# Feed-forwards: inverse deviations of the tokens applied to the up-projection's outputs instead of to the rows before the transposes

## The chip, the core and the metric

One core of one Trainium2 chip runs the whole program in one launch. The metric is the device time of an execution in microseconds (us), the median of several runs. The engines are named as the profile names them: PE (TensorE's matmuls), PEld (its weight loads), DVE (VectorE), ACT (ScalarE), POOL (GpSimd), SP (SyncE, which issues most transfers).

## What is computed

The reference runs 256 tokens of width 1024 through two models of two layers each, one after the other. Each layer is an attention and a feed-forward. The first two feed-forwards (`run_mlp`) are squared-ReLU MLPs. The last two (`run_ffn`) are what the change touches:

```
def conv_ffn(x, w_up, conv_w, conv_b, w_down):
    hdn = x @ w_up                       # 1024 -> 2 * 2816
    hdn = causal depthwise convolution of width 3 along the tokens(hdn) + conv_b
    gate, up = jnp.split(hdn, 2, axis=-1)
    return (jax.nn.gelu(gate, approximate=True) * up) @ w_down

h = h + rmsnorm(merge_heads(o) @ w_o, post_g)
f = conv_ffn(rmsnorm(h, ffn_pre_g[layer]), ...)
h = h + rmsnorm(f, ffn_post_g[layer])
```

`rmsnorm(h, g)` multiplies each token's row by its inverse deviation, 1 / sqrt(mean(h * h) + eps), and by the gain g. The inverse deviation is one number per token, so it can be applied before or after the matrix product; the convolution adds neighbouring tokens, so it must be applied before that.

## The kernel before

The tokens lie in two tiles of 128 (`t` = 0, 1). All weights are float32. A product is made of three matmuls in which each operand is split in a high and a low part: `split` (lines 162 to 190) writes the high part of a weight with ACT (`whi`, line 174) and the low part with DVE (`wlo`, line 175), a tile of 128x1024 at a time, in 8 buffers each.

`run_ffn` (lines 998 to 1023) does for each token tile: `op.run(t)`, the attention's output projection on PE; `add_post` (lines 492 to 503), which takes the inverse deviation of the projection's output and adds the normed rows to x (line 501); and `row_T` (lines 271 to 283), which multiplies x by the inverse deviation `x_rstd(t)` and by the gain's row (line 280, tile `y`), in two halves of 512 columns, and has PE transpose each half (`to_T`, line 257; evacuated by ACT at line 261, high part, and DVE at line 262, low part, tile `yT`). `x_rstd` (lines 232 to 245) is a chain: two squares with sums on ACT (line 236), two small DVE instructions (lines 238 and 240) and a power on POOL (line 222, tile `rstd`).

`conv_ffn` (lines 594 to 619) then goes through 11 groups `g` of 512 columns of the up-projection, two pairs (gate and up, `j` = 0, 1) of two chunks of 128 channels each. Group 0 goes through `up_tokens` (lines 533 to 549): the product with tokens on the partitions, an ACT copy out of PSUM (line 540, tile `ut`), PE transposes (line 543) and ACT copies (line 548). Groups 1 to 10 go through `up_pair` (lines 516 to 531): channels on the partitions, tokens along the row, evacuated by ACT (line 529) and DVE (line 530) into the tile `s`. The convolution follows: ACT scales and adds the bias (line 610, tile `cv`), DVE adds the two other taps (line 612, twice a chunk). Then come gelu (ACT, line 616), the product of gate and up (DVE, line 617) and the split of the result `u` (ACT line 512, DVE line 513). `Down` multiplies each `u` with the down-projection (lines 213 to 215) one group late, and takes the last three groups together at the end, tile t = 0 first, in the order 8, 9, 10.

The order of the instructions of each engine is laid out ahead of time by a scheduler that goes by the program's order and by when it reckons operands to be ready; each engine then runs its list strictly in order. Every 128x512 tile of the feed-forward's elementwise work comes from one pool of 5 buffers (tag `ev`).

`before_mlp` (lines 965 to 976), of the first two feed-forwards, already transposes rows that are multiplied by the gain alone (line 278) and takes the inverse deviation later. `along_rows` (lines 315 to 322) turns the two columns of inverse deviations into a row `R` of 256 on all partitions: two PE transposes (line 319) and a DVE copy (line 321); the attentions `layer_sb` and `layer_fox` use it.

Of the kernel before, what the change touches and what calls it, by code (L numbers as in the profile page):

```python
# [10 lines left out]
AF = mybir.ActivationFunctionType  # L11
ALU = mybir.AluOpType
PSUM = bass.MemoryType.PSUM

S, D, P = 256, 1024, 128
# [4 lines left out]
F2 = ((8 * D // 3 + 127) // 128) * 128  # L20
# [37 lines left out]
def body(ctx, tc, d, out):  # L58
    nc = tc.nc
    mm = nc.tensor.matmul  # L60
    act = nc.scalar.activation
    V = nc.vector
# [11 lines left out]
    def t512(name):  # L74
        return ap_.tile([P, 512], F32, name=name, tag="ev", bufs=E_BUFS)
# [7 lines left out]
    def acc_tile(i=0):  # L83

        tag = ("acc", "pt", "po")[i]
        return pp.tile([P, 512], F32, name="acc", tag=tag, bufs=1 if i else 2)

    def tp_tile(tag="ht"):
        return pp.tile([P, 4, P], F32, name="tp", tag=tag, bufs=2 if tag == "ht" else 1)

    def sc_tile():
        return pp.tile([P, 512], F32, name="sc", tag="sc", bufs=2)
# [20 lines left out]
    x = cst.tile([P, NT, D], F32, name="x")  # L113
# [118 lines left out]
    def row_rstd(lo, hi):  # L232

        ss = sm.tile([P, 2], F32, name="ss")
        for c, src in enumerate((lo, hi)):
            act(junk, src, AF.Square, accum_out=ss[:, c:c + 1])
        m0 = sm.tile([P, 1], F32, name="m0")
        V.tensor_scalar(m0, ss[:, 0:1], 1.0 / D, EPS, op0=ALU.mult, op1=ALU.add)
        ms = sm.tile([P, 1], F32, name="ms1")
        V.scalar_tensor_tensor(ms, ss[:, 1:2], 1.0 / D, m0, op0=ALU.mult, op1=ALU.add)  # L240
        return power(ms, 1)

    def x_rstd(t, src=None):
        src = x if src is None else src
        return row_rstd(src[:, t, :512], src[:, t, 512:])

    def yT_tiles():

        y = ap_.tile([P, KC, 2, S], F32R, name="yT", tag="yT", bufs=2)
        return y[:, :, 0], y[:, :, 1], y  # L250

    def to_T(dst, t, y, c0, g=None):

        n = y.shape[1] // P
        tp = tp_tile()
        for i in range(n):
            nc.tensor.transpose(tp[:, i, :], y[:, i * P:(i + 1) * P], ident)  # L257
        ts = slice(t * P, (t + 1) * P)
        if g is None:
            h, l = dst[0][:, c0:c0 + n, ts], dst[1][:, c0:c0 + n, ts]  # L260
            last = (act(h, tp[:, :n], AF.Copy),
                    V.tensor_tensor(l, tp[:, :n], h.bitcast(F32), op=ALU.subtract))
        else:
            for i in range(n):
                h, l = dst[0][:, c0 + i, ts], dst[1][:, c0 + i, ts]
                gk = g[:, c0 + i:c0 + i + 1]
                last = (act(h, tp[:, i], AF.Copy, scale=gk),
                        V.scalar_tensor_tensor(l, tp[:, i], gk, h.bitcast(F32), op0=ALU.mult, op1=ALU.subtract))
        return last

    def row_T(dst, t, xt, g=None, rows=None, scale=None):

        for c in range(2):
            y = xt[:, c * 512:(c + 1) * 512]
            if rows is not None:
                ys = t512("y")
                if scale is None:
                    V.tensor_tensor(ys, y, rows[c], op=ALU.mult)
                else:
                    V.scalar_tensor_tensor(ys, y, scale, rows[c], op0=ALU.mult, op1=ALU.mult)  # L280
                y = ys
            last = to_T(dst, t, y, 4 * c, g)
        return last
# [31 lines left out]
    def along_rows(rs):  # L315

        tp = tp_tile()
        for t in range(NT):
            nc.tensor.transpose(tp[:, t, :], rs[t].to_broadcast([P, P]), ident)
        R = cst.tile([P, S], F32, name="R", tag="R")  # L320
        V.tensor_copy(R, tp[:, :NT])
        return R
# [185 lines left out]
    def u_split(u):  # L508
        n_u[0] += 1
        hl = ap_.tile([P, 2, 512], F32R, name="u", tag=("q0", "q1", "k0", "k1")[n_u[0] % 4], bufs=1)  # L510
        hi, lo = hl[:, 0], hl[:, 1]
        act(hi, u, AF.Copy)  # L512
        V.tensor_tensor(lo, u, hi.bitcast(F32), op=ALU.subtract)  # L513
        return hi, lo

    def up_pair(yT, ws, o, j):

        s = t512("s")  # L520
        for i in range(2):
            b = sc_tile() if j == 0 else pp.tile([P, 512], F32, name="up", tag="ht", bufs=2)
            cs = slice(o + i * P, o + (i + 1) * P)
            for k in range(KC):
                mm(b, lhsT=ws[k][0][:, cs], rhs=yT[2][:, k].rearrange("p a s -> p (a s)"), start=k == 0, stop=False)  # L525
            for k in range(KC):
                mm(b[:, :S], lhsT=ws[k][1][:, cs], rhs=yT[0][:, k], start=False, stop=k == KC - 1)  # L527
            si = s[:, i * S:(i + 1) * S]
            act(si, b[:, S:], AF.Copy)
            V.tensor_tensor(si, b[:, :S], si, op=ALU.add)  # L530
        return s

    def up_tokens(yT, ws, f):

        pair = [None, None]
        for t in range(NT):
            acc = acc_tile()
            mm_rows(acc, yT, t, ws)
            ut = t512("ut")
            act(ut, acc, f)  # L540
            tp = tp_tile()
            for i in range(4):
                nc.tensor.transpose(tp[:, i, :], ut[:, i * P:(i + 1) * P], ident)
            for j in range(2):
                if t == 0:
                    pair[j] = t512("ur")
                pv = pair[j].rearrange("p (i s) -> p i s", s=S)
                act(pv[:, :, t * P:(t + 1) * P], tp[:, 2 * j:2 * j + 2], AF.Copy)
        return pair
# [41 lines left out]
                dn.put(u_split(u), g * 2 + j)  # L591
        dn.end()

    def conv_ffn(yT, w_up, cw, cb, w_down, finish, chain):
        nch = F2 // P
        dn = Down(w_down, nch // 2, finish)
        for g in range(nch // 2):
            ws = weights([(w_up, g * 256, 256, None), (w_up, F2 + g * 256, 256, None)],
                         after=chain if g == 1 else ())
            hs = up_tokens(yT, ws, AF.Copy) if g == 0 else [None, None]  # L600
            cs = []
            for j in range(2):
                s = hs[j]
                if s is None:
                    s = up_pair(yT, ws, j * 256, j)
                h = t512("cv")
                for i in range(2):
                    ch = j * nch + 2 * g + i
                    hi, pi = h[:, i * S:(i + 1) * S], s[:, i * S:(i + 1) * S]
                    act(hi, pi, AF.Identity, scale=cw(2, ch), bias=cb(ch))  # L610
                    for tap, sh in ((1, 1), (0, 2)):
                        V.scalar_tensor_tensor(hi[:, sh:], pi[:, :S - sh], cw(tap, ch), hi[:, sh:],  # L612
                                               op0=ALU.mult, op1=ALU.add)
                cs.append(h)
            u = cs[0]
            last_gelu[:] = [act(u, u, AF.Gelu_apprx_tanh)]
            V.tensor_tensor(u, u, cs[1], op=ALU.mult)
            dn.put(u_split(u), g)
        dn.end()
# [24 lines left out]
    ws = weights(kv_segs("a"), lambda: load_rows(mem, d["mem"], 1))  # L644
# [6 lines left out]
    ws = weights(kv_segs("b"))  # L651
# [344 lines left out]
        return nxt["yT"], nxt["r"], nxt["last"]  # L996

    def run_ffn(l, op, g_post):
        yT = yT_tiles()
        g = gbc(g_post)  # L1000
        rows = gain_rows(d["ffn_pre_g_2"][l])
        for t in range(NT):
            add_post(t, op.run(t), g)
            last = row_T(yT, t, x[:, t], rows=rows, scale=x_rstd(t))
        g2 = gbc(d["ffn_post_g_2"][l])
        nxt = {}

        def store(t, c):
            nc.sync.dma_start(out[0, t * P:(t + 1) * P, c * 512:(c + 1) * 512], x[:, t, c * 512:(c + 1) * 512])

        def finish(t, a):
            add_post(t, a, g2, store if l else None)
            if l == 0:
                if t == 0:
                    nxt["yT"], nxt["r"] = yT_tiles(), []
                last = row_T(nxt["yT"], t, x[:, t])
                nxt.setdefault("last", last)
                nxt["r"].append(x_rstd(t))
        nn = 2 * F2 // P
        ct = conv[l]  # L1020
        conv_ffn(yT, d["w_up_2"][l], lambda tap, ch: ct[:, tap * nn + ch:tap * nn + ch + 1],
                 lambda ch: ct[:, 3 * nn + ch:3 * nn + ch + 1], d["w_down_2"][l], finish, last)
        return nxt.get("yT"), nxt.get("r"), nxt.get("last")

# [33 lines left out]
```

## Time and profile before

| | |
|---|---|
| runs | 1243.33 us median of 3 (1241.75 to 1244.56) |
| the profiled execution's own time | 1243.45 us |
| its span | 1241.3 us |
| granted clock of TensorE, mean | 0.995 |
| busy share: PE, PEld, DVE, ACT, POOL | 98%, 82%, 73%, 61%, 4% |
| the two changed feed-forwards, first to last up-projection matmul | about 741 to 910 us and 1049 to 1218 us |

The span runs from the first to the last instruction; the profiled execution took 2.15 us more than its span. In a timeline row the first number is the start in us from the span's beginning, the second how long the row's instructions lasted, and a bracket at the end gives the idle time of that engine just before and what ended it. Matmuls are pipelined: the duration of one (0.39 us for 512 columns) is longer than the distance to the next, so distances are read from starts.

### The profile page before, as it was taken

To read this page: it belongs to the slowest core of one execution; us is meant where nothing else is said; L and a number is where in the kernel's file an instruction comes from. 1 tells how busy PE (TensorE), PEld (TensorE's weight loads), DVE (VectorE), ACT (ScalarE), POOL (GpSimd) and SP (SyncE) were. 2 spreads that over 40 slices of the span, in tenths; PEclk is the share of its full clock that TensorE was granted. 3 is DMA by queue.
4 is the path that set the end of the run, shared out by engine and by line. 5 is a ranking of instruction groups with operands and counts; after the bars stand their busy time and mean duration, and the time that the engine had idled before them with its cause. 6 is when DMAs were issued, how large, how long until landed. Compare 5 with 4: busy or idle time off the path is not lost.

```text
span 1241.3 us, 17829 instructions
## 1 busy us (share of the span) xinstructions
PE 1215.9 (98%) x6703; PEld 1022.2 (82%) x6703; DVE 906.0 (73%) x1677; ACT 753.1 (61%) x1363; POOL 44.2 (4%) x77
## 2 busy tenths in 40 slices
PE   8989999999999999999999999999999999999997
PEld 6867788888887788888889778888889987888886
DVE  5767757566777765756667888877788876987775
ACT  7655655454566655545556678666677755866663
POOL 1200000000000000000000010000001001000000
PEclk9998999999999999999999999999999999999999
DMA  9642356556453355645474426655637453565550
GB/s 323 220 169 88 117 174 210 193 172 234 134 182 127 103 203 185 214 177 187 153 237 154 136 63 206 207 180 194 203 114 237 149 160 113 196 206 178 180 191 34
DMA packets 125957, 214.21 MB, mean 173 GB/s; under 512 B 5280, under 2 KB 78304, under 8 KB 125872
## 3 DMA queue, kind: packets, MB, share of 16 engines
q1 hardware_dynamic: 123392, 207.25, 49.7%
q0 software_dynamic: 2336, 5.77, 1.7%
q8 instruction: 52, 0.85, 0.3%
q14 instruction: 33, 0.27, 0.1%
q10 hardware_dynamic: 144, 0.07, 0.0%
HBM read 211.96 MB, written 1.10 MB: 172 GB/s over the span
## 4 chain that ended last, share of the span: by engine, by line
PE 84%; issue 5%; DVE 4%; ACT 3%; POOL 1%; DMA 1%; SPq 0%; POOLq 0%; DVEq 0%; ACTq 0%
PE acc L213 12%; PE acc L214 12%; PE acc L215 12%; PE up L525 10%; PE sc L525 10%; PE up L527 5%; PE sc L527 5%; PE acc L292 3%; PE acc L293 3%; PE acc L295 3%; PE sc L365 2%; PE tp L405 2%; DVE wlo L175 2%; PE tp L453 1%; PE tp L257 1%
## 5 line engine op out<-in xcount | busy, mean ns | idle before, releaser
L175 DVE TENSOR_TENSOR wlo<-raw,whi 128x1024 fp32r<-128x1024 f32 x336 | 406.1, 1221 | 113.3 <-ACT whi L174 90.3
L174 ACT ACTIVATE whi<-raw 128x1024 fp32r<-128x1024 f32 x336 | 345.9, 1055 | 105.5 <-PE acc L215 60.7
L213 PE MATMUL acc<-whi,u 128*128 128x512 f32 x432 | 169.2, 392 | 0.0
L214 PE MATMUL acc<-wlo,u 128*128 128x512 f32 x432 | 168.7, 390 | 0.0
L215 PE MATMUL acc<-whi,u 128*128 128x512 f32 x432 | 168.0, 390 | 0.0
L525 PE MATMUL sc<-yT,whi 128*128 128x512 f32 x544 | 136.7, 391 | 0.0
L525 PE MATMUL up<-yT,whi 128*128 128x512 f32 x544 | 135.9, 392 | 0.0
L292 PE MATMUL acc<-whi,yT 128*128 128x512 f32 (+3 forms) x336 | 131.5, 394 | 0.0
L293 PE MATMUL acc<-wlo,yT 128*128 128x512 f32 (+3 forms) x336 | 129.4, 388 | 0.0
L525 PEld LDWEIGHTS sc<-yT,whi 128*128 128x128 f32 x544 | 99.7, 188 | 19.0
L525 PEld LDWEIGHTS up<-yT,whi 128*128 128x128 f32 x544 | 98.6, 189 | 18.2
L612 DVE SCALAR_TENSOR_TENSOR cv<-s,conv,cv 128x254 f32<-128x254 f32 (+1 forms) x160 | 76.2, 480 | 36.1 <-ACT cv L610 34.9
L215 PEld LDWEIGHTS acc<-whi,u 128*128 128x128 f32 x432 | 81.0, 188 | 17.9 <-DVE u L513 0.4
L213 PEld LDWEIGHTS acc<-whi,u 128*128 128x128 f32 x432 | 81.3, 188 | 16.3 <-ACT u L512 0.9
L214 PEld LDWEIGHTS acc<-wlo,u 128*128 128x128 f32 x432 | 81.3, 188 | 15.1
L295 PE MATMUL acc<-whi,yT 128*128 128x512 f32 (+3 forms) x336 | 83.0, 383 | 0.0
L185 DVE SCALAR_TENSOR_TENSOR wlo<-raw,g_late,whi 128x256 fp32r<-128x256 f32 (+4 forms) x128 | 68.2, 580 | 16.3 <-ACT whi L184 16.1
L527 PEld LDWEIGHTS up<-yT,wlo 128*128 128x128 f32 x544 | 74.2, 190 | 5.3
L527 PEld LDWEIGHTS sc<-yT,wlo 128*128 128x128 f32 x544 | 74.2, 190 | 5.2
L184 ACT ACTIVATE whi<-raw,g_late 128x256 fp32r<-128x256 f32 (+4 forms) x128 | 64.7, 578 | 20.3 <-PE acc L214 11.1
L527 PE MATMUL up<-yT,wlo 128*128 128x256 f32 x544 | 75.9, 282 | 0.0
L527 PE MATMUL sc<-yT,wlo 128*128 128x256 f32 x544 | 75.8, 282 | 0.0
(199 smaller groups left out, 1921.7 us busy)
## 6 DMA issues: line engine op xcount, KB each, us to landing
raw<-in_w_up SPq DMA_DIRECT2D x88, 512.0 KB, 4.4
raw<-in_w_down SPq DMA_DIRECT2D x22, 1024.0 KB, 5.0
raw<-in_a_w_up SPq DMA_DIRECT2D x16, 1024.0 KB, 5.3
raw<-in_a_w_down SPq DMA_DIRECT2D x16, 1024.0 KB, 5.0
raw<-in_b_w_up SPq DMA_DIRECT2D x16, 1024.0 KB, 5.3
raw<-in_b_w_down SPq DMA_DIRECT2D x16, 1024.0 KB, 4.9
raw<-in_sb_w_qkv SPq DMA_DIRECT2D x16, 512.0 KB, 5.1
raw<-in_a_w_in SPq DMA_DIRECT2D x6, 1024.0 KB, 6.0
```

The lines of the kernel that those rows point to most:

```text
L174: act(hv, rv[:, k0:k1], AF.Copy)
L175: V.tensor_tensor(lv, rv[:, k0:k1], hv.bitcast(F32), op=ALU.subtract)
L185: V.scalar_tensor_tensor(lv[:, k - k0, o:e], rv[:, k, o:e], gk, hv[:, k - k0, o:e].bitcast(F32), op0=ALU.mult, op1=ALU.subtract)
L213: mm(acc, lhsT=a[0], rhs=b[0], start=start, stop=False)
L214: mm(acc, lhsT=a[0], rhs=b[1], start=False, stop=False)
L215: mm(acc, lhsT=a[1], rhs=b[0], start=False, stop=stop)
L292: mm(acc, lhsT=h, rhs=ws[k][0], start=k == 0, stop=False)
L293: mm(acc, lhsT=h, rhs=ws[k][1], start=False, stop=False)
L295: mm(acc, lhsT=tslice(yT, k, t)[1], rhs=ws[k][0], start=False, stop=k == KC - 1)
L525: mm(b, lhsT=ws[k][0][:, cs], rhs=yT[2][:, k].rearrange("p a s -> p (a s)"), start=k == 0, stop=False)
L527: mm(b[:, :S], lhsT=ws[k][1][:, cs], rhs=yT[0][:, k], start=False, stop=k == KC - 1)
L612: V.scalar_tensor_tensor(hi[:, sh:], pi[:, :S - sh], cw(tap, ch), hi[:, sh:], op0=ALU.mult, op1=ALU.add)
```

## The change

`row_T` loses its parameter `scale`, so that the rows are multiplied by the gain alone. The inverse deviations are collected in a list `rs` and go to `conv_ffn`. In group 0 the ACT copy of `up_tokens` takes them as its scale (one number per token, tokens on the partitions). For the groups 1 to 10, `along_rows` makes a row `R` once per layer, and two POOL multiplies per pair bring it into `s` in place, between line 530 and line 610.

```diff
-    def row_T(dst, t, xt, g=None, rows=None, scale=None):
+    def row_T(dst, t, xt, g=None, rows=None):
...
                 ys = t512("y")
-                if scale is None:
-                    V.tensor_tensor(ys, y, rows[c], op=ALU.mult)
-                else:
-                    V.scalar_tensor_tensor(ys, y, scale, rows[c], op0=ALU.mult, op1=ALU.mult)
+                V.tensor_tensor(ys, y, rows[c], op=ALU.mult)
...
-    def up_tokens(yT, ws, f):
+    def up_tokens(yT, ws, f, rs=None):
...
-            act(ut, acc, f)
+            act(ut, acc, f, scale=1.0 if rs is None else rs[t])
...
-    def conv_ffn(yT, w_up, cw, cb, w_down, finish, chain):
+    def conv_ffn(yT, rs, w_up, cw, cb, w_down, finish, chain):
...
-            hs = up_tokens(yT, ws, AF.Copy) if g == 0 else [None, None]
+            hs = up_tokens(yT, ws, AF.Copy, rs) if g == 0 else [None, None]
+            R = along_rows(rs) if g == 0 else R
...
                     s = up_pair(yT, ws, j * 256, j)
+                    for i in range(2):
+                        si = s[:, i * S:(i + 1) * S]
+                        nc.gpsimd.tensor_tensor(si, si, R, op=ALU.mult)
...
     def run_ffn(l, op, g_post):
-        yT = yT_tiles()
+        yT, rs = yT_tiles(), []
...
-            last = row_T(yT, t, x[:, t], rows=rows, scale=x_rstd(t))
+            last = row_T(yT, t, x[:, t], rows=rows)
+            rs.append(x_rstd(t))
```

## Rows read from the trace of the kernel before

**Rows 1.** The page: engines' busy time, share of the span and instructions.

```profile
PE 1215.9 (98%) x6703; PEld 1022.2 (82%) x6703; DVE 906.0 (73%) x1677; ACT 753.1 (61%) x1363; POOL 44.2 (4%) x77
```

**Rows 2.** One line's instructions, 280: who waited for it (us, times).

```profile
  PE tp L257: 3.2, 4
```

**Rows 3.** Timeline, first changed feed-forward, t = 0, 736 to 738 us.

```profile
736.50 0.39 PE L214 MATMUL acc<-wlo,yT 128*128 128x512 f32 x1
...
737.41 0.66 PE L257 MATMUL tp<-con,y 128*128 128x128 f32 x4 [0.52 <-DVE y L280]
```

**Rows 4.** Timeline, the same feed-forward, t = 1, 743 to 749 us.

```profile
742.94 1.41 DVE L501 SCALAR_TENSOR_TENSOR x<-py,rstd,x 128x512 f32<-128x512 f32 x2
...
744.34 1.98 PE L295 MATMUL acc<-whi,yT 128*128 128x512 f32 x8
...
748.42 0.50 PE L292 MATMUL acc<-whi,yT 128*128 128x512 f32 x1
```

**Rows 5.** Timeline, second changed feed-forward, both tiles, 1041 to 1057 us.

```profile
1041.94 0.39 PE L213 MATMUL acc<-whi,yT 128*128 128x512 f32 x1
...
1043.10 0.66 PE L257 MATMUL tp<-con,y 128*128 128x128 f32 x4 [0.77 <-DVE y L280]
...
1052.28 1.29 PE L295 MATMUL acc<-whi,yT 128*128 128x512 f32 x5
...
1056.29 0.39 PE L292 MATMUL acc<-whi,yT 128*128 128x512 f32 x1
```

**Rows 6.** Timeline, first MLP: transposes of rows without the inverse deviation, 140 us.

```profile
140.51 0.60 PE L257 MATMUL tp<-con,y 128*128 128x128 f32 x4
...
141.18 0.39 PE L214 MATMUL acc<-wlo,yT 128*128 128x512 f32 x1
```

**Rows 7.** Timeline of PE, `along_rows` in the third attention, 643 us.

```profile
643.07 0.38 PE L319 MATMUL tp<-con,rstd 128*128 128x128 f32 x2
643.20 0.36 PE L213 MATMUL acc<-yT,whi 128*128 128x256 f32 x1
643.40 0.28 PE L214 MATMUL acc<-yT,whi 128*128 128x256 f32 x1
```

**Rows 8.** Groups by line and shape: copies with and without scale, multiply by R, POOL.

```profile
L465 ACT ACTIVATE vt<-acc,rstd 128x512 f32<-128x512 f32 x8 | 5.4, 680 | 6.3 <-PE acc L295 6.3
...
L540 ACT ACTIVATE ut<-acc 128x512 f32<-128x512 f32 x8 | 4.7, 593 | 4.5 <-PE acc L295 4.5
...
L844 DVE TENSOR_TENSOR kT<-acc,R 128x256 f32<-128x256 f32 x8 | 3.3, 416 | 0.0
...
L222 POOL TENSOR_TENSOR rstd<-ms,mhalf 128x1 f32<-128x1 f32 x28 | 18.2, 649 | 836.5 <-DVE ms L240 836.5
...
L175 DVE TENSOR_TENSOR wlo<-raw,whi 128x1024 fp32r<-128x1024 f32 x336 | 406.1, 1221 | 113.3 <-ACT whi L174 90.3 <-PE up L527 20.4
```

**Rows 9.** Timeline, second feed-forward's end: last chunk's chain, 1219 to 1224 us.

```profile
1219.41 0.42 DVE L530 TENSOR_TENSOR s<-up,s 128x256 f32<-128x256 f32 x1
1219.75 1.22 DVE L175 TENSOR_TENSOR wlo<-raw,whi 128x1024 fp32r<-128x1024 f32 x1
1219.87 0.60 ACT L610 ACTIVATE cv<-s,conv 128x256 f32<-128x256 f32 x1 [0.68 <-DVE s L530]
...
1224.05 0.19 PEld L215 LDWEIGHTS acc<-whi,u 128*128 128x128 f32 x1 [0.37 <-DVE u L513]
```

**Rows 10.** Timeline, first feed-forward's end: the same chain, 911 to 917 us.

```profile
911.57 0.42 DVE L530 TENSOR_TENSOR s<-up,s 128x256 f32<-128x256 f32 x1
...
912.66 0.60 ACT L610 ACTIVATE cv<-s,conv 128x256 f32<-128x256 f32 x1
...
916.52 0.19 PEld L213 LDWEIGHTS acc<-whi,u 128*128 128x128 f32 x1 [0.45 <-ACT u L512]
```

**Rows 11.** Busy time by engine in one steady group (us, instructions), 782 to 798.6 us.

```profile
782.00:798.60 16.60, 16.60 (x90) 14.32 (x89) 13.13 (x20) 10.89 (x18) 0.00 (x0) 1.00 0.61 204
```

**Rows 12.** Waits, 782 to 898 us (seven groups): us in total, times, longest.

```profile
DVE cv L612 <- ACT cv L610: 15.5, 20, 1.0
```

More of the change, by code (lines that the diff above doesn't have):

```diff
@@ L592, in mlp @@
         dn.end()
-    def conv_ffn(yT, w_up, cw, cb, w_down, finish, chain):
-        nch = F2 // P
+    def conv_ffn(yT, rs, w_up, cw, cb, w_down, finish, chain):
+        nch, R = F2 // P, None
         dn = Down(w_down, nch // 2, finish)
@@ L1020, in run_ffn @@
         ct = conv[l]
-        conv_ffn(yT, d["w_up_2"][l], lambda tap, ch: ct[:, tap * nn + ch:tap * nn + ch + 1],
+        conv_ffn(yT, rs, d["w_up_2"][l], lambda tap, ch: ct[:, tap * nn + ch:tap * nn + ch + 1],
                  lambda ch: ct[:, 3 * nn + ch:3 * nn + ch + 1], d["w_down_2"][l], finish, last)
```

## The prediction

> **What bounds the kernel now.** I read the page first, then the rows of line 280, then the timeline around each place where the change touches the code, then one steady group of the feed-forward. The page says that PE is the bound: busy for 98% of the span, while POOL is nearly idle [rows 1]. So the change can only win where PE stands still, and it can lose where it makes PE wait. Line 280, the multiply by inverse deviation and gain, has PE waiting for it four times, 3.2 us in all [rows 2]: once for each of two tiles in each of two feed-forwards. In the steady groups PE is busy for all of 16.60 us of each group, DVE for 13.13, ACT for 10.89, POOL for nothing [rows 11]. There the change adds work and takes nothing away.
>
> **What it removes.** The four waits, read from distances between starts of matmuls; matmuls of 512 columns follow each other at 0.227 us, since the eight of line 295 last 1.98 us, seven distances and one duration of 0.39 [rows 3, 4]. First feed-forward, t = 0: a matmul starts at 736.50, the next would at 736.73, and the transposes start at 737.41 [rows 3], so 0.68 us are lost. Second, t = 0: 1041.94 + 0.23 = 1042.17 against 1043.10 [rows 5], 0.93 lost. At t = 1 the lost time is seen from the last eight matmuls of the up-projection's t = 0 to the first matmul of its t = 1, with eight transposes between. Four transposes that do not wait cost PE 141.18 - 140.51 - 0.23 = 0.44 us [rows 6], so eight cost 0.88. First feed-forward: 744.34 + 1.82 + 0.88 = 747.04 against 748.42 [rows 4], 1.38 lost. Second: 1052.28 + 1.82 + 0.88 = 1054.98 against 1056.29 [rows 5], 1.31 lost. Sum: 0.68 + 0.93 + 1.38 + 1.31 = 4.3 us.
>
> Are the rows ready without the wait? At t = 1 of the first feed-forward, x is complete at 742.94 + 1.41 = 744.35 [rows 4]. Two multiplies by the gain follow, of about 0.7 us each like the two of line 501, so the first half can be transposed from about 745.1 and the second from 745.8, while PE still has line 295 to do until 746.16. ACT's evacuation of the first half, 0.6 us as for the copy of this shape [rows 8], ends before 747.04. The same distances hold in the second feed-forward. So I take all 4.3. The chain of `x_rstd` (ACT, DVE, POOL) remains, but what waits for it now is `ut` and `R`, which are needed a whole product later: nothing on PE stands behind it. DVE's multiply loses its scalar operand, which is worth less than 0.1 us each and lies beside PE.
>
> **What it adds.**
> **(a) `along_rows`, twice.** Its two transposes lie on PE. In the third attention they start at 643.07, the next matmuls at 643.20 and 643.40; without them these would start at 643.07 and, 0.12 us on, at 643.19 [rows 7]. So 0.2 us per layer, 0.4 in all. DVE's copy falls into the end of group 0, before POOL's first multiply, beside PE.
> **(b) The scaled copy in `up_tokens`, four times.** A copy of 128x512 with a scale per partition takes 680 ns, without it 593 [rows 8]: 0.09 us each. PE's transposes of `ut` come right behind it, in part filled with other matmuls: 0.2 us, bounds 0 and 0.35.
> **(c) 80 POOL multiplies of 128x256**, 40 per layer: ten groups, two pairs, two chunks. The trace has no such instruction on POOL. From below: DVE's multiply by R in this very shape, 0.42 us. From above: DVE's 128x1024 instruction with four times the columns, 1.22 us [rows 8]. A POOL power of one column takes 0.65 us [rows 8], which shows that POOL has a high price per instruction; I take P = 0.9 us, between that and the upper end. [...]
> In the steady groups `u` of a group is needed one group later, so 0.9 us in the chain from line 530 to line 610 has 16.60 us of cover. PSUM is free as soon as line 530 is done, and that stands ahead of the multiply. POOL itself has 4 x 0.9 = 3.6 us of work in 16.60. On POOL's queue nothing else falls into these groups; the powers of `add_post` come after the last multiply. No DMA moves. ACT and DVE work in order, so lines 610 and 612 now wait longer and what stands behind them waits too; the cover is the 3.5 us of a group in which DVE has nothing to do [rows 11]. I cost this at nothing; gone, it is the rival below.
> **(d) The end of each layer.** There the cover is gone: `u` of group 10 is used as soon as the products of groups 8 and 9 are done, and PE already waits for it, 0.37 us in the second layer and 0.45 in the first [rows 9, 10]. So each delay of that chain goes into the time, less what it meets of other waits. Second layer: the last line 530 ends at 1219.83, line 610 starts 0.04 later and ends at 1220.47, but DVE is in line 175 until 1220.97 [rows 9]: 0.50 us of slack. 0.94 - 0.50 = 0.44 us. First layer: line 530 ends at 911.99 and ACT, busy with other work, takes line 610 at 912.66 [rows 10]: 0.67 - 0.04 = 0.63 us of slack, 0.94 - 0.63 = 0.31 us. Sum 0.8 us; with P = 0.42 nothing, with P = 1.22 it is 1.4.
>
> **Sum:** -4.3 + 0.4 + 0.2 + 0.8 = -2.9 us. The profiled execution took 1243.45 us, 0.1 above the median of 1243.33, so 1240.6 us, or 1240.4 from the median.
>
> **Rivals.**
> 1. *POOL and DVE take turns (slower).* If a DVE instruction with two operands in SBUF and a POOL multiply exclude each other, DVE and POOL together have 13.13 + 3.6 = 16.73 us per group, more than PE's 16.60, which is 0.13 x 20 = 2.6 us. It decides from P = (16.60 - 13.13) / 4 = 0.87 us. At each end POOL would also wait for the line 175 in progress, until 1220.97 instead of 1219.87 [rows 9], 1.1 us, 2.2 for both. And DVE stands idle behind line 610 for 15.5 / 7 = 2.2 us of each group [rows 12]; if a tenth of it cannot be filled, that is 0.2 x 20 = 4. Together -2.9 + 2.6 + 2.2 + 4 = +5.9, 1249.4 us. For it: DVE is the busiest engine beside PE, and nearly all of its instructions there (lines 175, 612, 617, 513) read two tiles. Against it: with P under 0.87, or with the multiplies in DVE's idle time, it costs only the 2.2 at the ends. [...] No run here shows it: POOL's powers read one to four columns.
> 2. *POOL is cheap (faster).* With P = 0.42 the ends hide it and (b) is hidden too: -4.3 + 0.4 = -3.9, 1239.6 us. Against it: 0.65 us for a single column [rows 8].
> 3. *The stalls stay (the change does not do what it says).* If DVE's multiply by the gain is put in its list behind a line 175 of 1.22 us [rows 8] at each of the four places, the transposes come as late as before and only the additions are left: +1.4, 1244.9 us. Against it: the first MLP, whose rows carry the gain alone, has its transposes right behind a matmul [rows 6].
>
> **How the numbers follow.** A measurement of this kernel can tell about 0.2%, 2.5 us, from no change. The forecast gets 0.48. It lies just beyond that bound, and the unknown P and (b) move it by 0.9 to either side, so 0.28 of it is faster and 0.20 is no difference. Rival 2 gets 0.10, faster. Rival 1 gets 0.30: 0.26 slower, 0.04 within the bound, where only part of it comes. Rival 3 gets 0.12: 0.10 within the bound, 0.02 slower. Sums: faster 0.38, same 0.34, slower 0.28. The range: below, rival 2's 1239.6 less 0.6, since a median of few runs scatters (the runs before lie up to 1.6 under theirs), so 1239.0; above, rival 1's 1249.4. What is left out is rival 1 with P at 1.22, where DVE and POOL would need 18.0 us per group, and a part of rival 2's lower side. The forecast's own range is 1239.6 to 1242.
>
> **What would show it.** Right: no wait of PE for `y` before the transposes of either feed-forward; the two transposes of line 319's form once per feed-forward; the groups at 16.60 us; 80 POOL instructions of at most 1 us; a wait of PE for `u` of 0.7 to 0.9 us at both ends. Wrong: groups of more than 16.60 us; POOL multiplies or line 175 longer where they meet; DVE without idle time; transposes of `y` still behind a wait. If the time is above 1243 and the four waits are gone, the step that failed is (c) or (d).

## The result and the profile after

| | before | after |
|---|---|---|
| median of the runs | 1243.47 us | 1279.8 us (1279.26 to 1280.16) |
| ratio to before | 1 | 1.0289 [1.0277, 1.0302] |
| span of the profiled execution | 1241.3 us | 1278.4 us |
| granted clock of TensorE, mean | 0.995 | 0.989 |

The kernel became 2.9% slower, where 1240.6 us was forecast: the sign was wrong, and the time lies far above the range (1239.0 to 1249.4). Of the 37.1 us that the span grew, measured between the first matmuls of up-projections (line 522, before 525): the front of the first changed feed-forward gave 1.6 back; from group 1 to group 10 the two layers lost 8.7 and 9.2; from group 10 to the next layer's group 1 (the second front is in it) 9.75 were lost, and from the second layer's group 10 to the end 11.0. So half of it was lost in the steady groups, half at the ends of the layers.

The page of the kernel after: engines' busy time (compare [rows 1]), the chain that ended last, and three groups of instructions.

```profile
PE 1225.6 (96%) x6707; PEld 1027.3 (80%) x6707; DVE 918.1 (72%) x1679; ACT 748.0 (59%) x1363; POOL 119.0 (9%) x157
...
PE 58%; DVE 20%; ACT 8%; issue 8%; POOL 4%; DMA 1%; SPq 0%; DVEq 0%; POOLq 0%; ACTq 0%
...
L612 ACT ACTIVATE cv<-s,conv 128x256 f32<-128x256 f32 x80 | 47.8, 598 | 105.7 <-POOL s L607 105.7
L607 POOL TENSOR_TENSOR s<-s,R 128x256 f32<-128x256 f32 x80 | 72.6, 909 | 293.6 <-DVE s L527 293.6
```

No engine became the bound by its busy time: POOL's 80 multiplies are 72.6 us in all, DVE's work rose by 12 us (72% of the longer span, after 73%) and ACT's fell by 5. But ACT waited 105.7 us for POOL, and a third of the chain now goes through DVE, ACT and POOL. In the kernel before it was 8%:

```profile
PE 84%; issue 5%; DVE 4%; ACT 3%; POOL 1%; DMA 1%; SPq 0%; POOLq 0%; DVEq 0%; ACTq 0%
```

The waits of PE from 700 us on in the kernel after (in total, times, longest):

```profile
PE acc L213 <- ACT u L509: 16.6, 4, 7.4
PE sc L524 <- DVE wlo L175: 13.5, 12, 1.2
...
PE tp L257 <- DVE y L277: 0.2, 1, 0.2
```

The last line answers [rows 2]: the four waits for `y` are gone but for 0.2 us. Two new waits have come: PE waits for the low parts of the up-projection's weights, twelve times, and for `u` at the ends (in each layer 1.02 us for that of group 9, then over 7 us for that of group 10). The weights are late because DVE's list is late. One late group of the kernel after, busy time by engine in the columns of [rows 11]:

```profile
837.75:855.84 18.09, 16.88 (x90) 14.40 (x89) 13.59 (x20) 10.33 (x17) 3.12 (x5) 1.00 0.53 174
```

A group takes 18.09 us instead of 16.60, DVE is busy for 0.46 us more of it, and idle for 4.50 us instead of 3.47. A piece of the chain of waits through the same group (start, duration, what) shows where:

```profile
849.62 0.34 DVE s L527
849.97 0.07 issue
850.04 0.75 POOL s L607
850.79 0.03 issue
850.81 0.61 ACT cv L612
851.42 0.02 issue
851.45 0.49 DVE cv L614
851.94 0.03 issue
851.96 0.48 DVE cv L614
852.45 0.34 DVE s L527
```

The evacuation's sum on DVE (527), POOL's multiply (607), ACT's convolution (612), DVE's two taps (614), and then the next chunk's sum, which stands behind the taps in DVE's list: a ring. That second sum starts at 852.37, as the taps end, though PE had done its product by 846.44 and ACT its part by 851.68. PE does not occur in the ring. A turn of the ring is a whole group, from one group's product of gate and up on DVE to the next group's. Below are DVE's waits in a group before; then those of the group after, with its one longer instruction; then POOL's timeline of these places.

```profile
793.27 1.00 DVE L612 SCALAR_TENSOR_TENSOR cv<-s,conv,cv 128x255 f32<-128x255 f32 x2 [0.67 <-ACT cv L610]
...
795.46 1.00 DVE L612 SCALAR_TENSOR_TENSOR cv<-s,conv,cv 128x255 f32<-128x255 f32 x2 [0.67 <-ACT cv L610]
797.49 0.42 DVE L530 TENSOR_TENSOR s<-up,s 128x256 f32<-128x256 f32 x1 [1.03 <-ACT s L529]
798.93 0.48 DVE L612 SCALAR_TENSOR_TENSOR cv<-s,conv,cv 128x255 f32<-128x255 f32 x1 [1.01 <-ACT cv L610]
```

```profile
838.89 1.23 DVE L175 TENSOR_TENSOR wlo<-raw,whi 128x1024 fp32r<-128x1024 f32 x1 [1.37 <-ACT whi L174]
...
841.33 1.76 DVE L175 TENSOR_TENSOR wlo<-raw,whi 128x1024 fp32r<-128x1024 f32 x1
...
849.55 0.41 DVE L527 TENSOR_TENSOR s<-sc,s 128x256 f32<-128x256 f32 x1
851.45 1.00 DVE L614 SCALAR_TENSOR_TENSOR cv<-s,conv,cv 128x255 f32<-128x255 f32 x2 [1.49 <-ACT cv L612]
...
854.27 1.00 DVE L614 SCALAR_TENSOR_TENSOR cv<-s,conv,cv 128x255 f32<-128x255 f32 x2 [1.49 <-ACT cv L612]
```

```profile
841.10 0.91 POOL L607 TENSOR_TENSOR s<-s,R 128x256 f32<-128x256 f32 x1 [2.77 <-DVE s L527]
850.04 0.74 POOL L607 TENSOR_TENSOR s<-s,R 128x256 f32<-128x256 f32 x1 [8.03 <-DVE s L527]
```

Line 175 takes 1.76 us here, where it meets a multiply (1.22 otherwise [rows 8]), and the multiply 0.91 instead of 0.74. DVE's busy and idle times add up to the turn (13.59 + 4.50 = 18.09 us), and these rows say how it grew by 1.5 us: two waits behind POOL's multiply of 1.49 us instead of 0.67 (+1.64), the longer line 175 (+0.54), and at the third chunk one wait of 1.37 us where there were two, of 1.03 and 1.01 (-0.67), since the scheduler laid DVE's and ACT's lists out in another order there.

The end of the first changed layer, PE's timeline, and the granted clock (the number behind the engines) right behind the wait:

```profile
925.08 0.39 PE L213 MATMUL acc<-whi,u 128*128 128x512 f32 x1
932.63 0.79 PE L213 MATMUL acc<-whi,u 128*128 128x512 f32 x1 [7.16 <-ACT u L509]
933.22 0.63 PE L214 MATMUL acc<-wlo,u 128*128 128x512 f32 x1
933.65 0.63 PE L213 MATMUL acc<-whi,u 128*128 128x512 f32 x1
```

```profile
933.00:938.40 5.40, 5.40 (x14) 4.14 (x14) 1.22 (x3) 0.88 (x3) 0.00 (x0) 0.50 0.53 171
```

PE waits 7.16 us for the last `u`, where its weight loads waited 0.45 before [rows 10]; the second layer has 7.36. Behind the wait the granted clock is 0.50 for 5.4 us, where it was 1.00 in the group above: matmuls follow each other at 0.43 us instead of 0.23, and 13 of them cost 2.6 us more than at 0.23 (13 x 0.20).

### The profile page after: what moved, and what is told of

Read it like the earlier page. It is cut to its first block, busy times and chain, and to the rows that moved or that the text cites. A ratio compares the mean times of both kernels' runs of the same rounds, so it can differ in the third digit from the quotient of the medians.

```text
span 1278.4 us, 17945 instructions
## 1 busy us (share of the span) xinstructions
PE 1225.6 (96%) x6707; PEld 1027.3 (80%) x6707; DVE 918.1 (72%) x1679; ACT 748.0 (59%) x1363; POOL 119.0 (9%) x157
## 4 chain that ended last, share of the span: by engine, by line
PE 58%; DVE 20%; ACT 8%; issue 8%; POOL 4%; DMA 1%; SPq 0%; DVEq 0%; POOLq 0%; ACTq 0%
PE acc L213 9%; PE acc L214 9%; PE acc L215 9%; DVE wlo L175 9%; DVE cv L614 5%; PE sc L522 4%; PE up L522 4%; PE acc L290 4%; PE acc L289 4%; PE acc L292 3%; POOL s L607 3%; ACT whi L174 3%; ACT cv L612 2%; PE sc L362 2%; PE sc L524 2%
## 5 line engine op out<-in xcount | busy, mean ns | idle before, releaser
L175 DVE TENSOR_TENSOR wlo<-raw,whi 128x1024 fp32r<-128x1024 f32 x336 | 417.6, 1254 | 132.6 <-ACT whi L174 112.1
L174 ACT ACTIVATE whi<-raw 128x1024 fp32r<-128x1024 f32 x336 | 342.4, 1052 | 87.6 <-PE acc L215 41.1
L213 PE MATMUL acc<-whi,u 128*128 128x512 f32 x432 | 171.5, 397 | 16.6 <-ACT u L509 16.6
L215 PE MATMUL acc<-whi,u 128*128 128x512 f32 x432 | 170.0, 395 | 0.3 <-DVE u L510 0.3
L614 DVE SCALAR_TENSOR_TENSOR cv<-s,conv,cv 128x255 f32<-128x255 f32 (+1 forms) x160 | 77.0, 482 | 51.7 <-ACT cv L612 50.4
L612 ACT ACTIVATE cv<-s,conv 128x256 f32<-128x256 f32 x80 | 47.8, 598 | 105.7 <-POOL s L607 105.7
L607 POOL TENSOR_TENSOR s<-s,R 128x256 f32<-128x256 f32 x80 | 72.6, 909 | 293.6 <-DVE s L527 293.6
L524 PE MATMUL sc<-yT,wlo 128*128 128x256 f32 x544 | 79.1, 285 | 13.5 <-DVE wlo L175 13.5
```

Of the source, the lines that this page charges most:

```text
L174: act(hv, rv[:, k0:k1], AF.Copy)
L175: V.tensor_tensor(lv, rv[:, k0:k1], hv.bitcast(F32), op=ALU.subtract)
L213: mm(acc, lhsT=a[0], rhs=b[0], start=start, stop=False)
L215: mm(acc, lhsT=a[1], rhs=b[0], start=False, stop=stop)
L607: nc.gpsimd.tensor_tensor(si, si, R, op=ALU.mult)
```

## The experiments

All are the changed kernel with an edit. The times given are medians, with the ratio to the kernel before run beside it.

**1. No multiplies.** Lines 605 to 607 are taken out; the kernel leaves out the inverse deviation in the groups 1 to 10.

> The changed kernel without the 80 POOL multiplies: the chunks of groups 1 to 10 are left without the inverse deviation, all else is as changed. Both theories (the in-order wait on POOL's latency, and POOL and DVE blocking each other) put the whole loss on the multiplies, so both expect groups at 16.6 us again and only the gain at the fronts: 1238 to 1242 us against 1243.4 before. If it stays above 1250, the loss comes from elsewhere (the front, the scaled copy, the order of the lists).

1240.6 us, 0.9974 [0.9964, 0.9983]. All groups are back at 16.61 us, and PE waits for no `u`. The kernel is 3.1 us under the one before, the gain at the fronts, and the whole loss of 39 us belongs to the 80 multiplies, with the lists that the scheduler laid out for them.

**2. The multiplies on DVE.**

```diff
-                        nc.gpsimd.tensor_tensor(si, si, R, op=ALU.mult)
+                        V.tensor_tensor(si, si, R, op=ALU.mult)
```

> The 80 multiplies on DVE in the same place instead of on POOL. DVE gets 4 x 0.42 = 1.7 us more per group, 14.8 of 16.6. Latency theory: nothing waits on another engine between the sum and the multiply, the chain is longer by 0.35 us only, so groups stay at 16.6 us and the time is 1239 to 1245. Blocking theory: without POOL there is nothing to block, the same. If DVE's own load is what broke the groups, they stay near 18 us and the time near 1275.

1240.98 us, 0.9977 [0.9968, 0.9987]: within 0.4 us of no multiplies at all. One group by engine, from experiment 10, which is the same kernel again, and the one wait of DVE at the third chunk:

```profile
836.60:853.21 16.61, 16.61 (x89) 14.35 (x88) 14.47 (x25) 10.78 (x16) 0.00 (x0) 1.00 0.58 190
```

```profile
847.22 0.49 DVE L614 SCALAR_TENSOR_TENSOR cv<-s,conv,cv 128x255 f32<-128x255 f32 x1 [0.69 <-ACT cv L612]
```

DVE takes 14.47 us of work in the 16.61 without any loss. So DVE's busy time is not what POOL's multiplies ran into. But its list is in another order here: at the third chunk it waits 0.69 us, not 1.03 and 1.01, and the 1.35 us won by that are what the multiplies add to DVE's work (14.47 - 13.13 = 1.34). What DVE's multiplies cost in the old order was not measured.

**3. The multiplies on the side.** POOL writes its products into a tile that nobody reads.

```diff
-                        nc.gpsimd.tensor_tensor(si, si, R, op=ALU.mult)
+                        sd = o256()
+                        nc.gpsimd.tensor_tensor(sd, si, R, op=ALU.mult)
```

> All 80 POOL multiplies run, read the same two tiles and take the same time, but write to a tile that nobody reads; the convolution takes the unmultiplied chunk at once. Blocking theory: DVE's two-operand instructions are still held up, so most of the loss of 36 us stays (1265 or more). Latency theory: no instruction of ACT or DVE waits for POOL, so 1238 to 1244. In between, the split between the two is read from it.

1257.69 us, 1.0115 [1.0098, 1.0132], between the ranges of the two theories. The groups are at 16.61 again, but PE still waits for `u` at the ends, 5.75 and 5.72 us. The lists of PE, ACT and DVE hold the same instructions in the same order as in experiment 1, so the two traces can be laid upon each other. DVE in the same stretch of a group, first without multiplies, then with them on the side, and POOL's row:

```profile
815.58 0.47 DVE L611 SCALAR_TENSOR_TENSOR cv<-s,conv,cv 128x254 f32<-128x254 f32 x1
815.97 1.22 DVE L175 TENSOR_TENSOR wlo<-raw,whi 128x1024 fp32r<-128x1024 f32 x1
817.11 0.48 DVE L611 SCALAR_TENSOR_TENSOR cv<-s,conv,cv 128x255 f32<-128x255 f32 x1
```

```profile
818.42 0.47 DVE L615 SCALAR_TENSOR_TENSOR cv<-s,conv,cv 128x254 f32<-128x254 f32 x1
818.81 1.76 DVE L175 TENSOR_TENSOR wlo<-raw,whi 128x1024 fp32r<-128x1024 f32 x1
820.49 0.47 DVE L615 SCALAR_TENSOR_TENSOR cv<-s,conv,cv 128x255 f32<-128x255 f32 x1
```

```profile
818.65 0.84 POOL L608 TENSOR_TENSOR on<-s,R 128x256 f32<-128x256 f32 x1 [2.22 <-DVE s L527]
```

2.84 us behind ahead of the meeting, 3.38 after it: one meeting, 0.54 us. What became of these 0.54 is seen by following one instruction, the product of gate and up (line 619 in the kernel after), through groups 2 to 9 of the first layer; its starts in the two kernels, and the difference:

```
none     786.88  803.55  820.17  836.78  853.39  870.01  886.62  902.43
on side  789.34  806.45  823.55  840.66  857.77  874.89  892.01  908.32
behind     2.46    2.90    3.38    3.88    4.38    4.88    5.39    5.89
```

The first 2.46 us were lost in groups 1 and 2, where more instructions of DVE meet a multiply. From then on DVE and ACT fall 0.5 us further behind in every group and win nothing back. The idle 3.5 us of DVE do not absorb it, since in this order of the lists they are not slack: they are the hand-overs to ACT and back, and a turn of the ring without a meeting takes 17.11 - 0.54 = 16.57 us, as long as PE's group. While `u` has a group to spare PE does not notice; at the end of the layer it waits for all of it.

**4. The chain kept, POOL's work cut.** POOL multiplies 32 of the 256 columns of each chunk, in place, and ACT still waits for it.

```diff
-                        si = s[:, i * S:(i + 1) * S]
-                        nc.gpsimd.tensor_tensor(si, si, R, op=ALU.mult)
+                        si = s[:, i * S:i * S + 32]
+                        nc.gpsimd.tensor_tensor(si, si, R[:, :32], op=ALU.mult)
```

> The chain as changed (the convolution waits for POOL), but POOL multiplies only the first 32 of the 256 columns of a chunk; the other columns are left without the inverse deviation. Latency theory: POOL's instruction falls from 0.74 us to 0.2 to 0.3 us, and the groups are back near 16.6 us, time 1239 to 1248. If it is the mere handover to another engine, or the order of the lists that the extra step leads to, that costs, groups stay above 17.5 us and the time above 1260.

1257.12 us, 1.0113 [1.0097, 1.0128], between the two ranges again. Such a multiply takes 0.25 us alone. The ring's turn, by the starts of the product, is 16.91 us, the last distance 13.4 instead of 10.9, and PE waits 6.20 and 6.31 us at the ends. Meetings are nearly gone from the steady groups (line 175 takes 1.28 us at most there), so a short step in the chain is enough, and so is a meeting without any step in the chain (experiment 3). Take the distance from PE's start of a group to the product, less the same in experiment 1: the changed kernel's first layer is 7.7 us behind from group 5 to group 9, and there PE waits 1.2 us for line 175 in each group, and the groups grow longer. Up to group 9 of the first layer experiment 3 comes to 5.8 us, experiment 4 to 3.7 and experiment 5 to 2.8: neither the step nor the meetings alone get that far, the two together do.

**5. Multiplies that touch nothing of the chain.** They read the finished `u`, four behind each other, with PE's, ACT's and DVE's lists as in experiment 1.

```diff
-            dn.put(u_split(u), g)
+            us = u_split(u)
+            for i in range(4 if g else 0):
+                nc.gpsimd.tensor_tensor(o256(), us[0].bitcast(F32)[:, i % 2 * S:(i % 2 + 1) * S], R, op=ALU.mult)
+            dn.put(us, g)
```

> Left out: the inverse deviation in the groups 1 to 10. GpSimd makes the same number of multiplies of the same size, but they read the finished product u and write a tile that nobody reads; nobody of the chain waits for them, and the buffers of s are not held by them. The lists of PE, ACT and DVE are the same, row by row, as in the kernel without multiplies (1240.6). Theory (the ring): ACT and DVE hand each chunk to and fro, and one turn of that ring takes 16.57 us of the 16.61 that PE needs for a group; each two-input DVE instruction that meets a GpSimd multiply takes 0.55 more, the ring falls behind PE by as much, and what it is behind at the end of the layer PE waits for. Four multiplies follow each other behind each u, so 1 to 4 meetings per group: 0.5 to 2 us behind per group, a wait of PE of 5 us or more at each end, 1252 to 1275 in all. Rival (the multiplies held the tile s, or its buffers): no such wait, 1240 to 1242.

1251.7 us, 1.0065 [1.005, 1.008]: just under the range, with waits at the ends of under 4 us where 5 or more were expected, and the rival is out. It is not that the multiplies kept the tile `s` or its buffers. DVE's taps of the next chunk take 1.45 us for two where they meet the last of the multiplies, and 1.00 where they don't:

```profile
809.32 1.45 DVE L611 SCALAR_TENSOR_TENSOR cv<-s,conv,cv 128x255 f32<-128x255 f32 x2 [0.67 <-ACT cv L609]
...
811.78 1.00 DVE L611 SCALAR_TENSOR_TENSOR cv<-s,conv,cv 128x255 f32<-128x255 f32 x2 [0.67 <-ACT cv L609]
```

The turn is 16.94 us, 0.33 more than PE's group, and the waits at the ends are 3.63 and 3.57 us. The meeting is shorter than in experiment 3, and so is the wait. Without it this turn is 16.94 - 0.45 = 16.49 us, so the ring has 0.04 to 0.12 us of room in a group by the two experiments.

**6 and 7. POOL in some groups, DVE in the others.** First POOL in groups 8 to 10 only, then in 1 to 7 only.

```diff
-                        nc.gpsimd.tensor_tensor(si, si, R, op=ALU.mult)
+                        (nc.gpsimd if g > 7 else V).tensor_tensor(si, si, R, op=ALU.mult)
```

> GpSimd multiplies in the groups 8 to 10 only, DVE in the groups 1 to 7. Theory (the ring falls behind by a fixed amount per group that has GpSimd in it): groups stay at 16.61, the ring is behind by about 1.5 + 1.5 + 2.8 us at the end (the three last distances of the changed kernel less those without multiplies), so PE waits some 5 to 6 us at each end: 1251 to 1257. Rival (the loss at the end belongs to the last groups themselves, their multiplies beside back-to-back DVE work): the whole loss at the two ends of the changed kernel, 22 us, stays: 1260 to 1264.

> The reverse: GpSimd multiplies in the groups 1 to 7, DVE in the groups 8 to 10. Theory (the ring): seven turns of 18.08 put it some 10 us behind; about 5 of these PE waits for inside the groups, as in the changed kernel, and the rest is not won back by three turns with next to no slack: groups 4 to 7 longer than 16.61, and still a wait of 4 to 6 us at each end: 1258 to 1266. Rival (the loss at the end belongs to the last groups themselves): groups lose 2 x 4 to 5 us, no wait at the ends: 1248 to 1251.

The sixth: 1257.66 us, 1.0106 [1.0089, 1.0123], 0.7 over its theory's range and under its rival's; groups at 16.61, PE's waits 6.11 and 6.31. The seventh: 1268.5 us, 1.0204 [1.0189, 1.0219]; the groups grow to 18.09, from the fifth distance on in the first layer and the fourth in the second, and there are still waits of 4.40 and 4.58 although no multiply of POOL lies near the end. It is 2.5 us over its range: the groups lost 6.4 and 7.4 us, where about 5 a layer were expected. Both bear out that the loss is collected group by group, and not made at the end alone: three groups with POOL put the ring 5.8 us behind experiment 10 (0.8 in group 8, 2.3 in group 9, 2.8 in group 10, so the last ones cost more), and of the 6.4 us that seven put it behind 4.8 are still there three groups later.

**8. The order changed, POOL kept.** The convolution of a chunk is issued behind the evacuation of the next chunk, in ACT's and in DVE's list; `s` comes from a pool of 6 buffers that the feed-forward does not use otherwise.

```diff
+                    nxt = ev[2 * j + i + 1] if 2 * j + i + 1 < len(ev) else None
...
+                            order.enter_context(tc.issue_after(nxt[0].ins))
                         act(hi, pi, AF.Identity, scale=cw(2, ch), bias=cb(ch))
...
+                            order.enter_context(tc.issue_after(nxt[1].ins))
                         for tap, sh in ((1, 1), (0, 2)):
```

> GpSimd keeps all 80 multiplies, in place and in the chain. Only the order of ACT and DVE is changed: the convolution of a chunk (ACT and the two taps on DVE) is issued behind the evacuation of the next chunk, so that the multiply of a chunk lies beside the next chunk's evacuation; s comes from a pool of 6 other buffers. Theory (the ring's turn is a sum of hand-overs in a fixed order, and GpSimd's step of 0.74 us and two hand-overs lengthened it): the turn falls under 16.61, groups at 16.61, a wait of 0 to 3 us at each end from the multiplies that meet DVE: 1240 to 1249. Rival (GpSimd beside DVE costs whatever the order): at least the loss of the multiplies on the side, 1255 to 1260.

1249.19 us, 1.0046 [1.0031, 1.0061]. 30 of the 39 us are back, with all 80 multiplies in place on POOL. One group by engine, five groups together, and what is left of PE's waits for `u`:

```profile
837.04:853.65 16.61, 16.61 (x89) 14.34 (x88) 14.65 (x22) 11.17 (x17) 3.13 (x4) 1.00 0.61 195
803.82:886.88 83.06, 83.06 (x441) 71.69 (x440) 71.74 (x100) 51.14 (x80) 20.17 (x20) 1.00 0.61 192
```

```profile
PE acc L213 <- ACT u L509: 4.9, 2, 2.5
```

DVE is still held up (over the five groups 14.35 us busy a group against 13.13), POOL is busy for 4.03, and the group is still 16.61: with the chunks interleaved the ring has room. The order and the buffers of `s` changed together here; which of the two gives the room was not separated. What is left are 2.4 and 2.5 us at the ends and the clock behind them.

**9. The same with DVE for the last chunk of each group.** No next evacuation covers that chunk.

```diff
-                        nc.gpsimd.tensor_tensor(si, si, R, op=ALU.mult)
+                        (nc.gpsimd if j + i < 2 else V).tensor_tensor(si, si, R, op=ALU.mult)
```

> The changed order with GpSimd's multiplies for three chunks of four, and DVE's for the last chunk of each group, which no next evacuation covers. Theory (what the changed order left, 2.5 us at each end, is the last chunk's step through GpSimd beside the split of weights): waits of 0 to 1 us at the ends, 1240 to 1245. Rival (it is what the order itself does to the last groups): the waits of 2.5 us stay, 1248 to 1250.

1242.76 us, 0.9995 [0.9986, 1.0004]: waits of 1.0 and 1.1 us at the ends, level with the kernel before.

**10 to 12. DVE's multiplies, three forms.** Experiment 2 again; one multiply of 512 columns a pair (the edit below); and two in the order of experiment 8.

```diff
-                    for i in range(2):
-                        si = s[:, i * S:(i + 1) * S]
-                        nc.gpsimd.tensor_tensor(si, si, R, op=ALU.mult)
+                    s2 = s.rearrange("p (i s) -> p i s", s=S)
+                    V.tensor_tensor(s2, s2, R.unsqueeze(1).to_broadcast([P, 2, S]), op=ALU.mult)
```

> The kernel with the multiplies on DVE again, with more rounds, for a narrower interval: it gave 0.9977 [0.9968, 0.9987]. Theory (DVE's step needs no hand-over, so the ring of ACT and DVE keeps to PE's 16.61 and the waits at the fronts are saved): 1239.5 to 1242, the whole interval below 1. Rival (its gain was chance): an interval that holds 1.

> DVE multiplies a pair in one instruction of 512 columns (R read twice) in place of two of 256 columns. Two instructions of 0.42 become one of about 0.69, but the first chunk then waits for the second. Theory (the turn of the ring is a sum of hand-overs, and this one has fewer but later ones): groups at 16.61 or up to 0.2 above it, 1240 to 1246. Rival (only DVE's busy time counts): at or under the kernel with two multiplies a pair, 1240 to 1241.

> Multiplies on DVE, and the order in which the convolution of a chunk is issued behind the next chunk's evacuation. Theory (the ring is not the bound once DVE multiplies, and that order packs the last groups later): 1240 to 1246, no better than DVE's multiplies in the old order. Rival (the order itself gives ACT and DVE slack, which helps at the ends too): 1236 to 1240.

1240.63 us, 0.9978 [0.9969, 0.9987]; 1240.62, 0.9977 [0.9968, 0.9986]; 1240.29, 0.9973 [0.9963, 0.9984]. All three are a little faster than the kernel before, and cannot be told from each other: with PE busy throughout the groups there is nothing more to win there by the order. The eleventh lies in the ranges of both its theory and its rival and does not decide between them. With experiment 2 they are the complete versions that beat both kernels, by 0.2 to 0.3% of the kernel before.

## Why the prediction was wrong, step by step

**The removal of the four waits (-4.3 us): right, but for 0.6 us.** What was left of the waits for `y` is 0.2 us, and with (a) and (b), which the sum put at 0.6, it comes to -3.7; without multiplies the kernel gained 3.1, with DVE's 2.6 to 2.9. In the first layer of the changed kernel 1.6 us were gained at the front, where the steps give 0.68 + 1.38 - 0.3 = 1.8. In experiment 1 the distance from group 1 to group 2 is 0.3 us longer than before in each layer, where (a) put 0.2.

**(c), "I cost this at nothing": the step that failed.** P was not the mistake: the multiply takes 0.74 us alone, under the 0.9 taken (0.91 in the mean, with all meetings). That 0.65 us for a power of one column shows a high price per instruction was wrong for a multiply: one of 32 columns took 0.25 us. The mistake was the cover. "[T]he cover is the 3.5 us of a group in which DVE has nothing to do" took idle time for slack. [Rows 12] already said what most of these microseconds were, waits of DVE for ACT (2.2 us a group), and I used them in a rival only; the ring that they belong to turns in 16.49 to 16.57 us, and PE's group takes 16.61. The room was about 0.1 us a group at most, not 3.5. A multiply in the chain and a meeting with line 175 lengthened the turn to 18.09.

That `u` is needed one group later, so that 0.9 us in the chain "has 16.60 us of cover", was wrong in the same way: a delay that comes once is covered, one that comes in every group adds up.

**(d), 0.8 us for the two ends: wrong by a factor of about 25.** The chain of the last chunk was followed rightly, but from the point at which ACT and DVE stood before the change. They arrive there late: in the first layer DVE comes to the first chunk of group 10 11.15 us after PE's start of that group, where it was 4.92 before, and to the last chunk 20.97 us after it, where it was 12.56. PE's waits of 7.16 and 7.36, and the lower clock behind them (2.6 us, and about 2.0 in the second layer, where ten matmuls follow at 0.43 us), are about 19 us in all, and the two waits of 1.02 come on top.

**Rival 1 was right that POOL and DVE hold each other up, and wrong in its sum.** In experiment 3 line 175 took 1.76 us where it met a multiply, 0.54 more than without; the rows show the longer times, not what makes them longer. The prediction let only the later instruction wait; the multiply that was there first took 0.84 us instead of 0.74 as well. But the rival was worked out as a sum of busy times that decides from P = 0.87. The loss came with 0.74, where the sum is 13.13 + 4 x 0.74 = 16.09 us, under PE's 16.60. What decides is the turn of the ring, not the sum. The rival let a tenth of DVE's waits behind line 610 go unfilled; of all of DVE's idle time about 0.1 us a group could be filled. Its 2.2 us at the ends were again the last meeting alone, without those of the groups. And the range was cut where it should not have been: groups of 18.0 us were left out, as a case that needs P = 1.22.

**Rivals 2 and 3 did not come.** The sign that the prediction named (above 1243 with the four waits gone: (c) or (d)) pointed to the right place.

Left open: what the order of the lists contributes. The rows of DVE's list say how the 1.5 us of a turn divide, but in the changed kernel the order itself gave 0.67 us back, and experiments 2, 4 and 6 to 12 have lists that the scheduler laid out anew; only 1, 3 and 5 differ by the multiplies alone.

## What to carry to other kernels

Idle time of an engine is cover only if it is not the engine's share of a ring of hand-overs: follow one chunk from engine to engine until the same engine's next instruction, add up the turn, and compare that with the bound's time per group. A step added to a ring with no slack lengthens every turn, even while the bound does not show it, and the end of the loop pays for it (in the kernel after a turn of 18.09 us against 16.61, and 7.16 and 7.36 us of waits at the ends). When a cheap elementwise step must go into such a ring, try it on an engine that is already in it (DVE's 0.42 us cost nothing here, in the order that the scheduler then chose), or interleave the chunks first.

## What the hardware showed beyond that

Where a POOL multiply of two tiles met DVE instructions that read two tiles, one or both took longer: line 175 1.76 us instead of 1.22 and the multiply 0.84 instead of 0.74 (experiment 3), two taps 1.45 instead of 1.00 (experiment 5). Alone the multiply takes 0.74 us, and in the kernel after up to 2.64, at 759.62 us, where DVE's lines 614, 175 and 619 follow each other without a gap; the one of 32 columns, 0.25 us alone, took up to 2.16 (experiment 4's rows of its line):

```profile
L607 POOL TENSOR_TENSOR s<-s,R x80: 252/255/2162, 759.4 to 1231.6; 128x32 f32<-128x32 f32 x80
```

And a wait of PE cost more than its own length in some of these runs. In experiment 8, behind a wait of 2.41 us, the granted clock was 0.71 in the mean of the next 5.8 us (matmuls lie 0.43 us apart at first, from 921.63 us on 0.23), an estimated 5.8 x 0.29 = 1.7 us lost (first row); in experiment 9, behind a wait of 0.98 us, it stayed 1.00 (second row):

```profile
918.20:924.00 5.80, 5.80 (x19) 4.67 (x20) 2.01 (x6) 1.38 (x4) 0.23 (x1) 0.71 0.44 136
916.80:922.00 5.20, 5.20 (x23) 4.11 (x23) 2.69 (x6) 1.38 (x4) 0.55 (x1) 1.00 0.49 151
```
